# A merged schedule for a hybrid decoder trunk: MLP entry, down-projection and tail reordered, eight modulation tiles moved late

## The chip, the cores and the metric

One core of a Trainium2 chip runs the kernel. The time is the device time of one execution in microseconds (us), taken as the median of several; a profiled execution gives the trace from which everything else is read. The engines are TensorE (PE; weight loads are PEld), VectorE (DVE), ScalarE (ACT), GpSimd (POOL) and SyncE (SP), which here only issues DMA.

## The reference

One layer over 1024 tokens of width 1024, in float32. A conditioning vector gives six modulation vectors (shift, scale, gate for the mixer and for the MLP). The mixer joins causal pooling with chunked gated linear attention; then comes a gated MLP of 2 × 2816 channels with a causal convolution of width 3, and a last norm. Cut to what matters:

```python
mod = silu(c) @ ada_w + ada_b
sh1, sc1, g1, sh2, sc2, g2 = split(mod, 6)
h = rmsnorm(x) * (1 + sc1) + sh1
u, q, k, v, r, z = split(h @ w_in)
y = concat([pool_mixer(u), gla_mixer(q, k, v, r, z)]) @ w_out
x = x + g1 * y
h = rmsnorm(x) * (1 + sc2) + sh2
up = causal_conv3(h @ w_up) + conv_b
a, b = split(up, 2)
x = x + g2 * ((silu(a) * b) @ w_down)
out = rmsnorm(x) * final_norm
```

## The kernel before, in words

Channels lie on the 128 partitions, tokens along the free side, in two halves `hf` of 512 tokens (T = 512). Every large product is made of three fp32r matmuls per 128-channel block (high × high, high × low, low × high; `mm3`). For that each weight block is split on chip into a high part (a cast on ScalarE, L851) and a low part (a subtraction on VectorE, L852). All matmuls have line L107, so one goes by the names of their tiles: `pp` projections of the mixer, `gp` and `dg` gates and diagonal of the attention, `sc` its scores, `ss` sums of squares, `upx`, `upy`, `upz` the up-projection, `dn` the down-projection.

The order on TensorE is the order in which the code issues the matmuls. In the mixer this follows a clock of matmul time: side generators (`gates`, `gla_pair`, the norms) yield a delay in us of such time or a condition, and `tick` runs those that are due between the matmuls of the main jobs. The orders of the other engines and of SP's queue are made by the scheduling layer, within what data and buffers demand.

*Mixer.* `gates` (L317 on) makes from z the operand `le` (L320 to L322), yields 2.0, and then for each of two channel tiles does the product `gp`, a log-sigmoid on ScalarE and VectorE and a running sum `b` (L338). `gla_pair` begins, once `b`, k and q are there, with the differences of `b` on POOL (`le`, L359) and behind them the product of q and k on POOL (`le`, L402), which the diagonal product `dg` needs; then come exponentials on ScalarE (L363, L364), `kl` (L368) and `lq` (L371) on VectorE and the scores `sc`, over seven levels.

*Modulation.* 48 tiles of 128 × 1024 are loaded (512 KB each) and multiplied with the conditioning vector `cb`, spread over the partitions, by VectorE (L226), one sum per tile; a small operation (L232) stores it to `modv`. Tiles 16 to 47 run between the jobs of the mixer; the last eight, 40 to 47, are the gate of the MLP, which only the last residual sum uses (L1160).

*MLP up.* Each of 22 channel tiles takes seven products, numbered by kind (1, 2, 5, 6, 3, 7, 4), a scheme with sums and differences of the two token halves and of the two weight halves that needs seven products instead of eight. `order` is the list of steps (kind, i); the first RAMP = 6 tiles run kinds 1 and 2 before the rest. Step 4 ends a tile: convolution on VectorE (L987), Silu (L1043), product (L1046), store to `gd`, and a difference or sum of the halves on POOL (L862 or L1054) for the down-projection. `cb` in these steps (L994) is a tile's convolution input, another thing than the conditioning vector.

*MLP down.* The same scheme over p = 1, 2 and 5 mixed, 6 and 3 mixed, 7, 4, each of NJ = 11 steps; a step is four outputs of three matmuls each. `prepare_d` loads and splits operands three steps ahead. At the last step of a p the four sums are added to the residual tiles `xs` (L1160) or held (`hold`), squares go to `acc`, and the last step is cut into two halves of 256 tokens, after which sums, root (L1196, L1197), outputs (L1210, L1207, L1208) and stores (L1212) follow.

*Activation tables.* A table load on ScalarE (L189) stands before the first use of another set of functions; `exp_ln` (L187) loads the set of exponential and logarithm after a given instruction, here after the last Silu.

Of the kernel before, what the change touches and what calls it, by code (L numbers as in the profile page):

```python
# [26 lines left out]
ALU = mybir.AluOpType  # L27
# [26 lines left out]
def trunk_kernel(ctx, tc, xT, ccol, adaT, vecs, w_start, w_z, w_qkru, w_v, w_g2, w_pool,  # L54
# [165 lines left out]
    def mod_tile(t, a=None, late=None):  # L220
# [4 lines left out]
        with later(late):  # L225
            dve.scalar_tensor_tensor(out=a, in0=a, scalar=1.0, in1=cb, op0=ALU.mult,  # L226
                                     op1=ALU.mult, accum_out=acc)
# [90 lines left out]
    def gates(pz, hf):  # L318
# [4 lines left out]
        yield 2.0  # L323
# [70 lines left out]
    def gla_pair(hf, ct):  # L394
        b, k, q2 = bt[hf][ct], kt[hf][ct], qbd[hf][ct]
        pre = gla_prep(b, k, q2, LEVELS[0])
        attn = tmp("la", shape=(P, 4, 2, P))
        av = attn.rearrange("p c e t -> p (c e) t")
        qk = tmp("le")
        for hd in range(2):  # L400
            rr = slice(hd * 64, hd * 64 + 64)
            pool_e.tensor_tensor(out=qk[rr], in0=k[rr], in1=q2[rr, hd], op=ALU.mult)  # L402
        yield 3.0
# [109 lines left out]
    def gla_half(hf):  # L513
        for ct in range(2):
            yield lambda: all(x[hf][c] is not None for x in (bt, qbd, kt)
# [139 lines left out]
    mods = iter(range(16, 48))  # L655
# [61 lines left out]
    def jobs_out(hf):  # L717
# [24 lines left out]
        def evac(d, pp):  # L742
# [3 lines left out]
            if hf and d >= 4:  # L746
                sums[d - 4] = up_pool.tile([P, T], F32, tag="a22", name="s1", bufs=10)
                dve.scalar_tensor_tensor(out=sums[d - 4], in0=x1[1][d],
                                         scalar=modv[:, 32 + d:33 + d], in1=x1[1][d - 4],
                                         op0=ALU.mult, op1=ALU.add)  # L750
# [3 lines left out]
            nacc[hf] = sumsq_step(nacc[hf], d, x1[hf][d], pool_e, True, own)  # L754
# [242 lines left out]
    def seeded(src, prime):  # L997
# [353 lines left out]
```

## Time and profile before

| | |
|---|---|
| median of three runs | 1041.66 us (1040.40 to 1043.34) |
| profiled execution | 1043.22 us, span 1041.2 us |
| busy share of the span | PE 96%, PEld 79%, DVE 82%, ACT 52%, POOL 16% |
| memory traffic | 154.21 MB, mean 148 GB/s |

The span runs from the first to the last event of the trace; 2.0 us of the execution lie outside it. A row of the timeline shows start, duration, engine, line, operation, output and inputs, shape and count; brackets give how long the engine stood idle before it and what ended that. Rows of a stage table give, for a stretch, its length, busy time and count of each engine, the clock granted to TensorE (1.00 is full), the share of DMA engine time and GB/s.

### The profile page before, as it was taken

What the parts mean: (1) busy time and instruction counts of PE and PEld (TensorE: products, weight loads), DVE (VectorE), ACT (ScalarE), POOL (GpSimd) and SP (SyncE); (2) the same over time, 40 slices, a digit from 0 to 9 for tenths busy, and PEclk for the clock granted to TensorE, in tenths of its full rate; (3) what the DMA queues carried; (4) which work ended last, traced back from release to release, by engine and by line L of the source; (5) the groups of instructions that cost most, each with busy time, mean ns of one, the idle gap of its engine ahead of it and who ended that gap; (6) DMA issues with size and microseconds to landing.
All of it is one profiled execution on the core that took longest, in us unless ns stands there. A gap on an engine that the chain in (4) does not pass through costs nothing.

```text
span 1041.2 us, 12710 instructions
## 1 busy us (share of the span) xinstructions
PE 1002.2 (96%) x4507; PEld 819.5 (79%) x4507; DVE 848.8 (82%) x1212; ACT 541.9 (52%) x870; POOL 166.6 (16%) x156
## 2 busy tenths in 40 slices
PE   8989989999999999999999999999999999999995
PEld 6768767787787768877888888888888788888874
DVE  7967996889997949999878787777776675987884
ACT  4365575443633737665555555555554544644542
POOL 0035112223041120011101101101001000200210
PEclk9989989999999999999999999999999999999998
DMA  9823321455487441333222322333234787223542
GB/s 365 292 101 122 111 72 62 142 182 191 167 289 242 158 167 59 102 121 142 102 91 92 121 105 107 113 112 111 101 111 155 281 270 244 90 93 107 194 155 81
DMA packets 60815, 154.21 MB, mean 148 GB/s; under 512 B 6768, under 2 KB 9936, under 8 KB 60752
## 3 DMA queue, kind: packets, MB, share of 16 engines
q1 hardware_dynamic: 53904, 133.91, 37.3%
q0 software_dynamic: 4928, 17.30, 4.3%
q10 hardware_dynamic: 1920, 2.20, 0.7%
q8 instruction: 35, 0.57, 0.2%
q14 instruction: 28, 0.23, 0.1%
HBM read 127.69 MB, written 25.69 MB: 147 GB/s over the span
## 4 chain that ended last, share of the span: by engine, by line
PE 76%; DVE 12%; ACT 4%; DMA 4%; issue 2%; POOL 1%; SPq 0%; POOLq 0%; ACTq 0%; DVEq 0%
PE dn L107 18%; PE pp L107 16%; PE upy L107 15%; PE upx L107 11%; PE upz L107 10%; PE sc L107 2%; PE pr L107 2%; DVE ada L226 1%; DVE wl L158 1%; DVE xs L852 1%; PE ss L107 1%; DVE la L388 1%; DVE us L534 1%; POOL le L359 1%; DMA ua<-in_w_up_dram 1%
## 5 line engine op out<-in xcount | busy, mean ns | idle before, releaser
L107 PE MATMUL dn<-xs 128*128 128x512 f32 (+1 forms) x480 | 112.5, 390 | 1.7 <-DVE xs L852 1.3
L107 PE MATMUL dn<-ws 128*128 128x512 f32 x456 | 106.8, 390 | 2.0 <-DVE xs L1160 2.0
L107 PEld LDWEIGHTS dn<-xs 128*128 128x128 f32 x480 | 89.5, 190 | 21.3 <-DVE xs L852 2.1
L107 PEld LDWEIGHTS dn<-ws 128*128 128x128 f32 x456 | 85.8, 188 | 20.2 <-issue 2.4
L158 DVE TENSOR_TENSOR wl<-raw,wh 128x1024 fp32r<-128x1024 f32 (+1 forms) x49 | 62.6, 1277 | 31.9 <-ACT wh L156 31.8
L107 PE MATMUL upy<-sh,xs 128*128 128x512 f32 x264 | 86.6, 390 | 2.0 <-DVE cb L994 2.0
L107 PE MATMUL upy<-sh,ws 128*128 128x512 f32 x264 | 86.5, 390 | 0.0
L852 DVE TENSOR_TENSOR xs<-ua,xs 128x512 fp32r<-128x512 f32 x78 | 60.7, 783 | 14.8 <-ACT xs L851 14.8
L1047 POOL DMA_DIRECT2D gd<-y x22 | 12.0, 545 | 376.9 <-DVE y L1046 359.9
L156 ACT CAST wh<-raw 128x1024 fp32r<-128x1024 f32 (+1 forms) x49 | 50.4, 1029 | 39.5 <-PE pp L107 10.7
L107 PE MATMUL pp<-hh,wh 128*128 128x512 f32 x168 | 70.1, 417 | 0.5 <-ACT hh L285 0.5
L107 PE MATMUL pp<-hh,wl 128*128 128x512 f32 x168 | 66.7, 397 | 1.3 <-DVE wl L158 1.3
L852 DVE TENSOR_TENSOR ws<-ua,ws 128x512 fp32r<-128x512 f32 x76 | 55.3, 730 | 15.4 <-ACT ws L851 15.4
L107 PE MATMUL pp<-hl,wh 128*128 128x512 f32 x168 | 66.7, 397 | 0.5 <-DVE hl L287 0.4
L851 ACT CAST ws<-ua 128x512 fp32r<-128x512 f32 x76 | 47.1, 622 | 34.0 <-PE upy L107 17.3
L851 ACT CAST xs<-ua 128x512 fp32r<-128x512 f32 x78 | 48.1, 622 | 30.5 <-PE upy L107 17.4
L107 PE MATMUL upx<-hh,xs 128*128 128x512 f32 x192 | 63.3, 395 | 0.0
L862 DVE TENSOR_TENSOR ua<-ua 128x512 f32<-128x512 f32 x88 | 60.3, 690 | 2.1 <-DMA ua<-in_w_up_dram 0.2
L107 PE MATMUL upz<-sh,ws 128*128 128x512 f32 x184 | 60.4, 390 | 0.0
L987 DVE SCALAR_TENSOR_TENSOR y<-ca,vec,y 128x1023 f32<-128x1023 f32 (+1 forms) x44 | 56.4, 1281 | 4.4 <-ACT y L984 3.5
L107 PEld LDWEIGHTS upy<-sh,xs 128*128 128x128 f32 x264 | 49.6, 188 | 13.0 <-DVE cb L994 2.8
L987 DVE SCALAR_TENSOR_TENSOR y<-cb,vec,y 128x1023 f32<-128x1023 f32 (+1 forms) x44 | 56.3, 1280 | 2.4 <-ACT y L984 2.1
(259 smaller groups left out, 2482.5 us busy)
## 6 DMA issues: line engine op xcount, KB each, us to landing
ua<-in_w_up_dram SPq DMA_DIRECT2D x49, 512.0 KB, 3.3
ada<-in_adaT_dram SPq DMA_DIRECT2D x32, 512.0 KB, 3.3
gd<-y POOLq DMA_DIRECT2D x22, 512.0 KB, 2.9
da<-gd SPq DMA_DIRECT2D x36, 256.0 KB, 2.9
da<-in_w_down_dram SPq DMA_DIRECT2D x36, 256.0 KB, 3.3
raw<-in_w_qkru_dram SPq DMA_DIRECT2D x17, 512.0 KB, 3.5
raw<-in_w_out_dram SPq DMA_DIRECT2D x16, 512.0 KB, 4.1
x<-in_xT_dram SPq DMA_DIRECT2D x24, 256.0 KB, 4.2
```

Source lines behind the costliest of these rows:

```text
L107: pe.matmul(out=out, lhsT=lhsT, rhs=rhs, start=start, stop=stop, skip_group_check=more)
L156: act.copy(out=wh, in_=raw)
L158: mark["wl"] = dve.tensor_tensor(out=wl, in0=raw, in1=wh.bitcast(F32), op=ALU.subtract)
L226: dve.scalar_tensor_tensor(out=a, in0=a, scalar=1.0, in1=cb, op0=ALU.mult, op1=ALU.mult, accum_out=acc)
L359: pool_e.tensor_tensor(out=e.rearrange("p (n h) -> p n h", n=nb), in0=b.rearrange("p (n h) -> p n h", n=nb), in1=bb[:, :, 0, h - 1:h].broa ...
L388: dve.copy_predicated(out=av.rearrange("p a (n two h) -> p a n two h", two=2, h=h)[:, :, :, 1], mask=cit[:, mi].rearrange("p (n h) -> p n ...
L534: dve.tensor_tensor(out=n[:, lo:], in0=a[:, lo:], in1=a[:, lo - sh:16 + T - sh], op=ALU.add)
L851: act.copy(out=h, in_=src)
L852: dve.tensor_tensor(out=l, in0=src, in1=h.bitcast(F32), op=ALU.subtract)
L862: eng.tensor_tensor(out=out, in0=a, in1=b, op=ALU.subtract)
L987: dve.scalar_tensor_tensor(out=y[:, sh:], in0=c[:, :S - sh], scalar=cw[j], in1=y[:, sh:], op0=ALU.mult, op1=ALU.add)
L1047: nc.gpsimd.dma_start(out=gd[i], in_=ya)
```

## The change

It joins several edits.

- `gates` yields 3.0 in the first half and 4.5 in the second. `gla_pair` does the product of q and k before it waits for `b`.
- In the output projection of the second half the four sums follow the last tile, and the last adds of squares are on VectorE. Modulation tiles 40 to 47 no longer run in the mixer; `cb` is stored to memory. The Silu table is loaded after the second norm's exponential.
- In the MLP step (4, i − 1) stands one product later. Silu and what follows are kept back (`gated`) until the copy that seeds a later tile; differences and sums are on VectorE instead of POOL, those of the first six tiles from reloaded products.
- In the down-projection the exponential table is loaded after p = 1's held copies; `cb` and the eight tiles are loaded and multiplied from step 8 on (`late_mods`); p = 4's operands are loaded six steps ahead into buffers of their own; residual sums are formed as soon as an output is ready (`done`).
- In the tail the last two steps are cut in two halves, all of the first before the second; four of the eight outputs of a half are made by one 4 × 256 operation from tiles scaled before, and no output is made on ScalarE or POOL.

POOL at the start of the attention of the first half; `le<-k,lb` is the product of q and k, `le<-b` the differences of `b`. Before:

```order
L304 MEMSET lb 64x512
L359 ISA
L359 TENSOR_TENSOR le<-b 128x512
L402 TENSOR_TENSOR le<-k,lb 64x512 x2
L415 TENSOR_TENSOR lm<-b 128x512
L359 TENSOR_TENSOR le<-b 128x512 x2
```

and now:

```order
L304 MEMSET lb 64x512
L399 ISA
L399 TENSOR_TENSOR le<-k,lb 64x512 x2
L359 TENSOR_TENSOR le<-b 128x512 x2
L417 TENSOR_TENSOR lm<-b 128x512
L241 TENSOR_TENSOR nsa<-nsa,nsq 128x512
```

The product has moved ahead of the first operation on `b`.

VectorE in p = 1 of the down-projection; `xs` and `ws` are splits of the operands `ra`, `rb` and `da` of coming steps, `ada` the modulation products. Before:

```order
L852 TENSOR_TENSOR xs<-rb,xs 128x512
L852 TENSOR_TENSOR ws<-ra,ws 128x512
L852 TENSOR_TENSOR ws<-rb,ws 128x512
L862 TENSOR_TENSOR ra<-da,ra 128x512
L862 TENSOR_TENSOR rb<-rb_6958,rb 128x512
L852 TENSOR_TENSOR ws<-ra,ws 128x512
L852 TENSOR_TENSOR ws<-rb,ws 128x512
```

and now:

```order
L858 TENSOR_TENSOR ws<-rb,ws 128x512
L226 SCALAR_TENSOR_TENSOR ada,macc<-ada,cb 128x1024
L858 TENSOR_TENSOR ws<-ra,ws 128x512
L232 SCALAR_TENSOR_TENSOR modv<-macc,vec 128x1
L226 SCALAR_TENSOR_TENSOR ada,macc<-ada,cb 128x1024
L858 TENSOR_TENSOR xs<-da,xs 128x512 x2
L232 SCALAR_TENSOR_TENSOR modv<-macc,vec 128x1
L226 SCALAR_TENSOR_TENSOR ada,macc<-ada,cb 128x1024
L858 TENSOR_TENSOR ws<-rb,ws 128x512
```

The first modulation products stand between the splits of the last steps of p = 1 and of the first of p = 2.

TensorE at the end of the kernel; `ss<-acc` is the sum of the squares collected so far and `ss<-sq` that of one output tile. The difference, with − for before and + for now:

```order
 L107 MATMUL dn<-ws 128x512 x24
-L107 MATMUL dn<-xs 128x512 x12
-L107 MATMUL dn<-xs 128x256 x12
+L107 MATMUL dn<-xs 128x256 x42
 L107 MATMUL ss<-acc,ones 128x256
-L107 MATMUL dn<-xs 128x256 x12
+L107 MATMUL dn<-xs 128x256 x6
+L107 MATMUL ss<-sq,ones 128x256 x2
 L107 MATMUL ss<-acc,ones 128x256
-L107 MATMUL ss<-sq,ones 128x256 x8
```

All 48 products of the last two steps are now 256 wide, the first half's sum stands six matmuls ahead of the last product, and eight sums of single tiles have become three.

The diff, cut to its core:

```diff
-        yield 2.0
+        yield 4.5 if hf else 3.0
...
     def gla_pair(hf, ct):
-        b, k, q2 = bt[hf][ct], kt[hf][ct], qbd[hf][ct]
-        pre = gla_prep(b, k, q2, LEVELS[0])
-        attn = tmp("la", shape=(P, 4, 2, P))
-        av = attn.rearrange("p c e t -> p (c e) t")
+        k, q2 = kt[hf][ct], qbd[hf][ct]
         qk = tmp("le")
         for hd in range(2):
             rr = slice(hd * 64, hd * 64 + 64)
             pool_e.tensor_tensor(out=qk[rr], in0=k[rr], in1=q2[rr, hd], op=ALU.mult)
+        yield lambda: bt[hf][ct] is not None
+        b = bt[hf][ct]
+        pre = gla_prep(b, k, q2, LEVELS[0])
...
-    mods = iter(range(16, 48))
+    mods = iter(range(16, 40))
...
-            nacc[hf] = sumsq_step(nacc[hf], d, x1[hf][d], pool_e, True, own)
+            nacc[hf] = sumsq_step(nacc[hf], d, x1[hf][d], dve if hf and d >= 4 else pool_e,
+                                  True, own)
+            if hf and d == 7:
+                for e in range(4):
...
+    cbd = tc.dram_tile([P, NK * P], F32, name="cbd")
+    nc.sync.dma_start(out=cbd, in_=cb)
...
-    run_jobs(jobs_out(0), 2)
+    run_jobs(jobs_out(0), 1)
...
     for i in range(NFF):
-        order += [(1, i)] if i >= RAMP else [(5, i)]
-        order += [(4, i - 1)] if i else []
-        order += [(5, i), (2, i)] if i >= RAMP else []
-        order += [(6, i), (3, i), (7, i)]
+        done = [(4, i - 1)] if i else []
+        if i < RAMP:
+            order += [(5, i), (6, i)] + done + [(3, i), (7, i)]
+        else:
+            order += [(1, i), (5, i)] + done + [(2, i), (6, i), (3, i), (7, i)]
...
         r = rstd_of(nacc[1], s2)
+        with tc.issue_after(mark["exp"].ins):
+            act.preload_act_table_set("silu_and_others")
...
-        for _ in range(2):
+        for _ in range(2 if n else 0):
             next(second, None)
...
+    def gated():
+        while pend:
+            i, ya, yb = pend.pop(0)
+            with tc.issue_after(mark["seed"].ins):
+                act.activation(out=ya, in_=ya, func=AF.Silu)
+            dve.tensor_tensor(out=ya, in0=ya, in1=yb, op=ALU.mult)
             nc.gpsimd.dma_start(out=gd[i], in_=ya)
+            if RAMP <= i < 2 * RAMP:
+                a, b = small("s3"), small("s3")
+                nc.sync.dma_start(out=a, in_=gd[i - RAMP][:, 0:T])
+                nc.sync.dma_start(out=b, in_=gd[i - RAMP][:, T:])
+                sub(dve, a, a, b)
+                nc.gpsimd.dma_start(out=s3d[i - RAMP], in_=a)
...
+    def load_ahead(n):
+        if n < len(steps) and steps[n][0] == 4:
+            j = steps[n][1]
+            ahead[j] = blk("a4"), blk("b4")
+            ld(ahead[j][0], a_src(22, j))
+            ld_b(ahead[j][1], 21, j)
...
+        if p == 1:
+            last = hold(1, d, pp)
+            if d == 3:
+                exp_ln(last)
...
+    def finish_half(lo, order):
+        n = T // 2
         ss = bank("ss")[:, 0:n]
+        for d in order:
+            sq = acc[1][:, lo:lo + n] if d is None else acc[d, lo]
+            mm(ss, ones, sq, d == order[0], d == order[-1])
+        r = rstd_out(ss, n)
+        o = dn["o"].tile([P, 4, n], F32, tag="o", name="o", bufs=4)
+        dve.tensor_tensor(out=o, in0=xs_tail[:, :, lo:lo + n],
+                          in1=r.unsqueeze(1).broadcast_to([P, 4, n]), op=ALU.mult)
+        store(nc.scalar if lo else nc.sync, 1, 4, 4, lo, n, o)
+        outputs(1, lo, n, r, 0, 4)
...
+    def late_mods():
+        def big(name):
+            return dn["o"].tile([P, NK * P], F32, tag="o", name=name, bufs=4)
+        c = big("cb")
+        ld(c, cbd)
+        got = []
+        for t in range(40, 48):
+            a = big("ada")
+            ld(a, adaT[t])
+            got.append((t, a))
+            if len(got) < 3 and t < 47:
+                continue
+            yield
+            t1, a1 = got.pop(0)
+            mod_tile(t1, a1, c=c)
+            yield
```

More of the change, by code (lines that the diff above doesn't have):

```diff
@@ L514, in gla_half @@
         for ct in range(2):
-            yield lambda: all(x[hf][c] is not None for x in (bt, qbd, kt)
+            yield lambda: all(x[hf][c] is not None for x in (qbd, kt)
                               for c in ((ct,) if hf else (0, 1)))
@@ L1166, in down_mm @@
         ah, al = flat(ah), flat(al)
+        if p == 7 and 3 <= j < 7:
+            evac(1, j + 1, held[5, j - 3])
+        if p == 4 and j < 4:
+            x = xs[1][4 + j]
+            act.activation(out=x, in_=x, func=AF.Copy, scale=vec[:, V_FN + 4 + j:V_FN + 5 + j])
         if p in (1, 5) and j == 0:
@@ L1170, in down_mm, with hold, done @@
         more = p not in (1, 5)
-        cuts = ((0, T // 2), (T // 2, T // 2)) if p == 4 and j == NJ - 1 else ((0, T),)
-        for lo, n in cuts:
-            for d in range(4):
-                mm3(pp[d][:, lo:lo + n], bh[:, d], bl[:, d], ah[:, lo:lo + n], al[:, lo:lo + n],
-                    not more and j == 0, j == NJ - 1, more)
-            if n < T:
-                finish_last(pp, lo, n)
-        return pp
+        for d in range(4):
+            mm3(pp[d], bh[:, d], bl[:, d], ah, al, not more and j == 0, j == NJ - 1, more)
+            if j == NJ - 1:
+                done(p, d, pp[d], 0, T)
+    held = {}
+    def hold(p, d, pp):
+        held[p, d] = dn["o"].tile([P, T], F32, tag="hold", name="hold", bufs=8)
+        return act.copy(out=held[p, d], in_=pp)
+    def done(p, d, pp, lo, n):
+        if p == 1:
+            last = hold(1, d, pp)
+            if d == 3:
+                exp_ln(last)
+        elif p == 5:
+            hold(5, d, pp)
+        elif p == 2:
+            evac(0, d, pp)
+            act.copy(out=pp, in_=held[1, d])
+            squares(0, d)
+        elif p == 6:
+            evac(0, 4 + d, pp)
+        elif p == 3:
+            evac(0, 4 + d, pp)
+            squares(0, 4 + d)
+        elif p == 7:
+            evac(1, 4 + d, pp)
+            squares(1, 4 + d)
+        else:
+            sq = acc[d, lo] = square(evac(1, d, pp, lo, n), "sq", n)
+            if d < (1 if lo else 4):
+                a = acc[1][:, lo:lo + n]
+                dve.tensor_tensor(out=a, in0=a, in1=sq, op=ALU.add)
     acc = {}
@@ L1248, in trunk_kernel @@
     for n in range(EARLY, len(steps)):
-        prepare_d(n + 3)
+        p, j = steps[n]
+        load_ahead(n + 6)
+        if n >= 8:
+            next(late, None)
+        if j < NJ - 1:
+            prepare_d(n + 3)
         if n >= 2 * NJ - 2 and n % 2 == 0 and x_loads:
@@ L1252, in trunk_kernel @@
             ld(xs[hf][d], x1d[hf][d])
[L1253 to L1254 removed]
+        if p < 5 and p > 3 and j >= NJ - 2:
+            continue
+        down_mm(p, j)
+        if j == NJ - 1:
+            prepare_d(n + 3)
         if (p, j) == (7, 3):
             finish_first()
[L1257 to L1280 removed]
+    finish_last()
 def _tiles(w):
```

128 lines of the change are left out of this document (57 added, 71 removed).

## The prediction

> **What bounds the kernel now.** I read the page first, then the busy time by stage, then each place where TensorE stands still. The page's first rows, its clock row and the shares of the chain:
>
> ```profile
> PE 1002.2 (96%) x4507; PEld 819.5 (79%) x4507; DVE 848.8 (82%) x1212; ACT 541.9 (52%) x870; POOL 166.6 (16%) x156
> PEclk9989989999999999999999999999999999999998
> PE 76%; DVE 12%; ACT 4%; DMA 4%; issue 2%; POOL 1%; SPq 0%; POOLq 0%; ACTq 0%; DVEq 0%
> ```
>
> TensorE sets the end: it is idle for 1041.2 − 1002.2 = 39.0 us, and it runs below full clock here and there. An edit that leaves the matmuls nearly as they are can win only those 39 us and what the low clock costs. The stages (columns: length, then busy time of PE, PEld, DVE, ACT, POOL, the granted clock, DMA share, GB/s):
>
> ```profile
> 60.00:110.00 50.00, 46.62 (x219) 38.48 (x218) 39.74 (x46) 28.50 (x53) 27.16 (x20) 0.93 0.28 96
> 110.00:200.00 90.00, 82.71 (x399) 66.94 (x397) 75.17 (x129) 52.18 (x89) 18.07 (x17) 0.96 0.26 91
> 600.00:806.00 206.00, 206.00 (x911) 170.72 (x910) 156.90 (x191) 109.18 (x163) 26.55 (x33) 1.00 0.32 115
> 826.00:976.00 150.00, 150.00 (x659) 123.89 (x659) 120.18 (x182) 74.53 (x132) 13.22 (x7) 1.00 0.50 166
> 1024.00:1041.20 17.20, 6.30 (x37) 5.43 (x35) 8.65 (x22) 6.01 (x14) 1.45 (x2) 0.82 0.37 122
> ```
>
> The long stretches of the MLP have no idle TensorE at all, with VectorE at 157 of 206 and 120 of 150 us. So an operation moved to VectorE there has cover, and nothing is to be won there. What can be won is in the mixer, at the seams and in the tail. Narrow windows show the low clock, each right behind a stop of TensorE:
>
> ```profile
> 72.50:79.20 6.70, 6.70 (x19) 5.45 (x20) 6.70 (x9) 4.36 (x9) 4.58 (x4) 0.50 0.12 39
> 147.60:154.30 6.70, 5.64 (x13) 4.48 (x14) 6.25 (x12) 3.85 (x8) 0.00 (x0) 0.50 0.20 73
> 386.50:389.80 3.30, 3.30 (x6) 1.66 (x5) 2.36 (x4) 0.50 (x1) 0.00 (x0) 0.50 0.34 103
> 823.40:826.70 3.30, 3.30 (x10) 2.54 (x9) 2.88 (x5) 0.36 (x1) 0.00 (x0) 0.50 1.02 395
> ```
>
> At half clock a busy us does half a us of work, so these cost 3.35, 2.8, 1.65 and 1.65 us: half of the PE column. A stop that goes takes its half-clock stretch with it.
>
> **The change, part by part.** Gains are negative.
>
> *First half, gates and q·k.* Rows of the timeline (start, duration, engine, line, operation; in brackets the idle time before it and what ended it):
>
> ```profile
> 62.50 0.50 PE L107 MATMUL gp<-le,g2w 96*128 96x512 f32 x1 [0.81 <-ACT le L322]
> 67.43 1.87 POOL L359 TENSOR_TENSOR le<-b 128x512 f32<-128x512 f32 x1 [17.17 <-DVE b L338]
> 69.26 2.68 POOL L402 TENSOR_TENSOR le<-k,lb 64x512 f32<-64x512 f32 x2
> 70.74 1.75 DVE L371 TENSOR_TENSOR lq<-lb,le 128x512 f32<-128x512 f32 x1
> 71.99 1.27 PE L107 MATMUL dg<-hsel,le 128*128 128x2 f32 x7 [2.58 <-POOL le L402]
> ```
>
> The product that `dg` waits for (2.68) stands on POOL behind an operation that needs `b` and comes after a 17.17 us wait. Moved ahead of it, it needs only k and q; POOL has nothing else then, so it is done well before 67. `gp`, three matmuls later, meets its operand. That removes 0.81 + 2.58 + 3.35 = 6.7. What is late next: the scores `sc`, which need `lq`, ready at 70.74 + 1.75 = 72.5. Without its stops TensorE comes there at about 70.8: `gp` at 62.5, then 35 full matmuls at 0.224 (36.00 us for 161 records at 862 to 898, below) and the small `dg`. `lq` itself should be quicker when POOL is quiet, so I leave a stop of about 1.3 and a part of a half-clock stretch: −4.5, between −1.5 and −6.7.
>
> *Second half.*
>
> ```profile
> 148.04 0.57 ACT L322 CAST le<-pp 32x512 fp32r<-32x512 f32 x1
> 148.66 0.80 PE L107 MATMUL gp<-le,g2w 96*128 96x512 f32 x1 [2.66 <-ACT le L322]
> 168.77 0.51 PE L107 MATMUL pp<-wh,hh 128*128 128x512 f32 x1 [1.73 <-ACT k L312]
> ```
>
> `gp` waits for a cast queued on ScalarE behind other work. The gate now yields 4.5 instead of 2.0, and in the built order `gp` stands 16 matmuls (3.6 us) later, more than the 2.66 stop. At most −(2.66 + 2.8) = −5.5; at worst the same queue stops the next product and nothing is won. Nearer the first, since other matmuls fill the place: −4.0. The 1.73 at 168.77 is a k copy behind the queue of the exponentials; with POOL's work in another order it goes or stays: −1.0 (0 to −1.7).
>
> *Sums of the second half of the residual, and the second norm.*
>
> ```profile
> 384.32 1.58 POOL L241 TENSOR_TENSOR nsa<-nsa,nsq 128x512 f32<-128x512 f32 x1 [0.38 <-ACT nsq L237]
> 385.95 1.60 PE L107 MATMUL ss<-nsa,ones 128*128 128x512 f32 x2 [2.23 <-POOL nsa L241]
> ```
>
> The last adds go to VectorE, the four sums behind them, and `ss` stands twelve matmuls later (2.7 us), more than its 2.23 wait. Gain 2.23 + 1.65 = 3.9; I take −3.6 (0 to −3.9). The preload of the Silu table costs 1.28 on ScalarE (row below) ahead of the ramp's products, which have that much room.
>
> *Gated products of the MLP.*
>
> ```profile
> 459.34 2.20 DVE L852 TENSOR_TENSOR xs<-ua,xs 128x512 fp32r<-128x512 f32 x1
> 459.67 1.30 POOL L862 TENSOR_TENSOR y<-y 128x512 f32<-128x512 f32 x1
> 462.19 0.50 PE L107 MATMUL upy<-sh,xs 128*128 128x512 f32 x1 [1.13 <-DVE cb L994]
> 476.93 0.50 PE L107 MATMUL upy<-sh,xs 128*128 128x512 f32 x1 [0.85 <-DVE cb L994]
> ```
>
> While POOL subtracts, VectorE's split takes 2.20 instead of 0.68 (the same form at 994.19, below). All 22 such POOL operations go to VectorE, where the same work costs 0.69 (993.58, below): 15 us over the 425 us of the MLP's up part, which has a quarter of VectorE free. The six earliest products are read back from memory (12 loads of 256 KB), at some 110 GB/s of traffic. Step (4, i−1) comes one product later, which also gives `cb` time. −1.8 (0 to −2.0); +4 if the cover were gone (six stops of 0.69).
>
> *Start of the down-projection.*
>
> ```profile
> 818.72 1.28 ACT L189 ACT_TABLE_LOAD   x1
> 820.02 0.62 ACT L851 CAST xs<-rb 128x512 fp32r<-128x512 f32 x1
> 820.69 0.73 PE L107 MATMUL dn<-xs 128*128 128x512 f32 x2 [0.37 <-ACT xs L851]
> 822.72 2.82 PE L107 MATMUL dn<-xs 128*128 128x512 f32 x7 [1.30 <-DVE xs L852]
> ```
>
> The table load stands between the last Silu and the cast that TensorE waits for, and POOL's last add slows the split. The load moves behind p = 1, where nothing waits for it; the cast comes 1.28 earlier. All is 0.37 + 1.30 + 1.65 = 3.3; −3.0 (0 to −3.3).
>
> *Start of p = 4.*
>
> ```profile
> 993.58 0.69 DVE L862 TENSOR_TENSOR da<-da,rb 128x512 f32<-128x512 f32 x1 [0.98 <-DMA da<-in_w_down_dram]
> 994.19 0.68 DVE L852 TENSOR_TENSOR xs<-da,xs 128x512 fp32r<-128x512 f32 x1
> 995.68 0.70 PE L107 MATMUL dn<-ws 128*128 128x512 f32 x2 [2.00 <-DVE xs L1160]
> ```
>
> VectorE's subtraction waits for a load, and the evacuation that frees a bank stands behind it. With the loads six steps ahead and evacuation first: −1.8 (+1 to −2.0).
>
> *The two-half tail.*
>
> ```profile
> 1026.25 0.59 PE L107 MATMUL ss<-acc,ones 128*128 128x256 f32 x2
> 1029.56 2.86 DVE L1210 SCALAR_TENSOR_TENSOR o<-xs,vec,r 128x256 f32<-128x256 f32 x7 [2.52 <-ACT r L1197]
> 1036.79 0.38 ACTq L1212 DMA_DIRECT2D out_dram<-o  x1
> ```
>
> From the end of the products (1026.25) both roots, then the output operations, 0.41 each (2.86 / 7), go one after the other, the last store is issued at 1036.8 and lands by 1041.2. In the change the first half's sum stands ahead of the last six narrow matmuls, so its root is there about 0.6 us after the products. VectorE then needs per half one 1024-wide product (1.2, as the 1.27 of the modulation row below) and four of 0.41: 5.7 in all, with some evacuations between. The last is done about 6.7 after the products, where the last store stood 10.5 after them: −3.8 (−2.5 to −4.5). Cutting a second step in two puts 24 more 256-wide matmuls for 12 fewer 512-wide: +0.2.
>
> *The eight modulation tiles.* Columns of the first row: busy, mean ns of one, idle before.
>
> ```profile
> L226 DVE SCALAR_TENSOR_TENSOR ada<-ada,cb 128x1024 f32<-128x1024 f32 x32 | 40.3, 1266 | 3.6 <-DMA ada<-in_adaT_dram 3.4
> 826.00:862.00 36.00, 36.00 (x158) 29.76 (x158) 26.33 (x43) 16.83 (x30) 0.00 (x0) 0.99 0.88 295
> 862.00:898.00 36.00, 36.00 (x161) 29.82 (x160) 26.08 (x42) 17.27 (x31) 1.27 (x1) 1.00 0.63 212
> 898.00:920.00 22.00, 22.00 (x99) 18.23 (x98) 22.00 (x32) 13.26 (x26) 5.78 (x3) 1.00 0.13 48
> ```
>
> They leave the mixer, where TensorE rarely waits for them: 0. In the built order they stand among the splits from p = 1 on, here about 826 to 862. There they add 8 × 1.27 = 10.1 us to VectorE (26.3 of 36 busy, so 36.4: full), and nine 512 KB loads, 4.7 MB, to a stretch that moves 295 GB/s × 36 us = 10.6 MB; at the 395 GB/s of 823 to 827 it could move 14.2, so 1.1 MB, 3 us, slides behind. Cover: operands are split three steps (8 us) ahead, part of those loads are residual tiles needed only at about 894, and 862 to 898 has 10 us of VectorE free. Queued behind a modulation that waits for its load are the splits of the coming steps, and behind the loads on SP the weights of p = 2 and 5. At 898 to 920 VectorE is full without any of it. Bounds: 0 with the cover, +11 without; I take +1.5, nearer the first.
>
> *At nothing:* the store of the conditioning vector (512 KB, in the mixer at 91 GB/s); the four rescaling copies in p = 4, on ScalarE at half its time (74.5 of 150); the outputs' issue on SP, which has by then no load left to issue. Without cover each is one operation of 0.6, or 1.7 for the store, once.
>
> **Sum:** −4.5 − 4.0 − 1.0 − 3.6 − 1.8 − 3.0 − 1.8 − 3.8 + 0.2 + 1.5 = −21.8. The profiled execution took 1043.2 (2.0 outside its span), so 1021.4 on its basis; the median of the runs shown is 1.56 below it: 1041.66 − 21.8 = 1019.9, say **1020 us**. My bounds of the terms, not all at once, make its own range 1011 to 1025.
>
> **Rivals.** *The mixer's stops only move.* Its late operand is then the next one: `lq` at 72.5, ScalarE's queue at 148. For: VectorE is busy 75 of 90 us at 110 to 200. Against: the operand waited for at 71.99 sits behind unrelated work. The 9.5 of the mixer shrink to 2: 1020 + 7.5 = 1027.
>
> *The tiles take VectorE's cover.* It enters 898 to 920, already 22.00 of 22, with a backlog of up to 10 us, and TensorE stands for that: about 1030. For: 36.4 of 36. Against: 862 to 898 has room to catch up.
>
> *Slower than before.* The same place, with the memory queue: each of the eight tiles brings a stop of the 1.27 modulation and a late 512 KB load (1.8 us at 295 GB/s). That is 3.1 us each, over the 2.2 us after which a half-clock stretch stood at 386, so 1.65 more: 8 × 4.7 = 38 us, 1020 − 1.5 + 38 = 1056. It decides only once VectorE's lead of three steps is used up.
>
> *The stops are not what lowers the clock.* The half-clock stretches then stay, and of the gains only the idle time remains: 3.35 + 2.8 + 1.65 + 1.65 = 9.5 less, about 1029. Against: all four stand right behind stops of 1.3 to 2.7 us. [...]
>
> **How the numbers follow.** Forecast 0.60, mixer's stops move 0.19, VectorE's cover 0.09, clock stays 0.04, slower 0.04, and 0.04 for more than the sum (the mixer's full 13.9 instead of 9.5, and the others at their far ends: 1009). Range 1009 to 1032. About 0.3%, 3 us, is what can be told from no change: faster 0.94, same 0.02, slower 0.04.
>
> **What would show it.** Right: `dg` with no wait for POOL and the clock at 1.00 from 72 to 79; no half clock at 386 and 823; `upy` without stops for `cb`; 826 to 976 without idle TensorE; the last store about 7 us behind the last product. Wrong: `sc` waiting 2 us or more for VectorE; `gp` still behind ScalarE; `dn` waiting for `xs` or `ws` splits around 840 to 920, with VectorE full and the modulations waiting for their loads.

## The result

The changed kernel takes 1026.17 us (median of 4 runs, 1024.54 to 1026.31), the kernel before beside it 1042.50 (4 runs, 1040.40 to 1044.39). The ratio is 0.984, with a 95% interval of 0.9818 to 0.9863: 16.3 us faster, where 1020 had been predicted, 21.7 us faster. The profiled execution of the change took 1026.08 us with a span of 1024.3.

First the rows of its page that answer to those of before: the engines' busy time and the clock.

```profile
PE 995.5 (97%) x4509; PEld 811.7 (79%) x4509; DVE 849.5 (83%) x1239; ACT 540.8 (53%) x871; POOL 128.0 (13%) x128
PEclk9999999999899999999999999999999999999998
```

TensorE is idle for 1024.3 − 995.5 = 28.8 us instead of 39.0, and the other 6.7 of the 16.9 us between the spans are busy time that fell, which is mostly less time at half clock: 6.8 us ahead of the tail instead of 23.9. Ahead of the tail the clock row has one digit below 9, the 8 of the slice from 256 to 282 us: that is the start of the out-projection, below. The group of the down-projection's weight products (busy, mean ns, then idle before) shows a waiter that it did not have: VectorE's weight splits.

```profile
L107 PE MATMUL dn<-ws 128*128 128x512 f32 x456 | 108.2, 391 | 2.2 <-DVE ws L858 2.1
```

The best ledger is by stages of TensorE's work, from the start of one product to the start of another as the timeline gives them (us):

| from … to | before | after | change | predicted |
|---|---|---|---|---|
| first `gp` … first out product `pp<-yh` | 205.69 | 196.56 | −9.1 | −9.5 |
| … first `upx` | 112.65 | 115.04 | **+2.4** | 0 |
| … first `upz` | 38.81 | 34.64 | −4.2 | −3.6 |
| … last `upz` | 383.76 | 381.03 | −2.7 | −1.8 |
| first `dn` … last `dn` | 219.79 | 220.85 | **+1.1** | −3.1 |
| last `dn` … end | 15.07 | 10.62 | −4.5 | −3.8 |

Two stages hold more than the whole miss: 2.4 lost in the out-projection, where nothing had been forecast, and 4.2 in the down-projection; the other four together gained 1.8 more than forecast. The stages of the change (columns as before the prediction's stage table):

```profile
60.00:110.00 50.00, 46.50 (x232) 37.75 (x232) 41.03 (x53) 29.53 (x56) 28.82 (x20) 1.00 0.30 96
110.00:200.00 90.00, 88.53 (x436) 71.36 (x435) 79.62 (x132) 55.44 (x96) 18.63 (x18) 1.00 0.33 108
200.00:270.00 70.00, 63.59 (x298) 51.71 (x297) 64.61 (x109) 33.08 (x57) 16.47 (x9) 0.96 0.54 175
...
812.00:848.00 36.00, 36.00 (x161) 29.81 (x160) 31.78 (x61) 18.21 (x31) 0.00 (x0) 1.00 0.96 349
848.00:884.00 36.00, 36.00 (x161) 29.81 (x160) 29.22 (x47) 16.22 (x29) 1.38 (x1) 1.00 0.83 279
884.00:906.00 22.00, 20.59 (x90) 16.51 (x89) 22.00 (x32) 13.41 (x26) 5.67 (x3) 1.00 0.38 130
906.00:962.00 56.00, 54.72 (x234) 42.79 (x233) 49.58 (x76) 23.36 (x43) 6.16 (x4) 1.00 0.52 165
```

From 60 to 200 the clock is full. In 200 to 270 it is 0.96 and 6.4 us are idle. In the down-projection TensorE keeps its pace until 884, beside a VectorE that has to do 31.78 of 36, and loses it in the next 22 us, where VectorE is full. The count of matmuls says more there than the idle time, since a matmul behind a stop is drawn longer (0.50 us in several rows below, where the mean of the group above is 391 ns): it is compared below.

**The start of the attention.** Rows of TensorE and POOL:

```profile
61.10 2.61 POOL L399 TENSOR_TENSOR le<-k,lb 64x512 f32<-64x512 f32 x2 [10.73 <-ACT k L312]
...
66.66 0.95 PE L107 MATMUL dg<-hsel,le 128*128 128x2 f32 x8
...
72.23 1.16 PE L107 MATMUL sc<-lq,kl 128*128 128x128 f32 x8 [0.38 <-DVE lq L371]
...
78.70 1.16 PE L107 MATMUL sc<-lq,kl 128*128 128x128 f32 x8 [1.19 <-DVE lq L371]
...
88.06 2.02 DVE L158 TENSOR_TENSOR wl<-raw,wh 128x1024 fp32r<-128x1024 f32 x1 [2.45 <-ACT wh L156]
...
90.14 0.50 PE L107 MATMUL pp<-wl,hh 128*128 128x512 f32 x1 [1.32 <-DVE wl L158]
```

The product of q and k is done at 63.7 and `dg` waits for nothing. The scores wait twice for `lq`, and a weight split that takes 2.02 beside POOL's sums of squares stops TensorE for another 1.32.

**The start of the out-projection.** ScalarE and then TensorE:

```profile
263.41 1.28 ACT L453 ACT_TABLE_LOAD   x1
264.70 0.58 ACT L529 COPY us<-pp 128x512 f32<-128x512 f32 x1
...
265.34 0.80 PE L107 MATMUL pp<-yh,wh 128*128 128x512 f32 x1 [3.96 <-ACT us L529]
```

The copy that frees the bank of this product (the piece of accumulator memory that it fills) has a table load ahead of it on ScalarE. In the kernel before, the same product waited too, at 270, but there the table load stood behind the copy:

```profile
271.44 0.67 ACT L552 ACTIVATE yh<-po,vec 128x512 fp32r<-128x512 f32 x1
272.01 0.57 ACT L527 COPY us<-pp 128x512 f32<-128x512 f32 x1
...
273.55 1.28 ACT L451 ACT_TABLE_LOAD   x1
...
272.63 0.50 PE L107 MATMUL pp<-yh,wh 128*128 128x512 f32 x1 [2.24 <-ACT us L527]
```

**The down-projection at 885.** VectorE, TensorE and POOL:

```profile
885.21 1.79 DVE L858 TENSOR_TENSOR ws<-ra,ws 128x512 fp32r<-128x512 f32 x1
886.92 1.75 DVE L858 TENSOR_TENSOR ws<-rb,ws 128x512 fp32r<-128x512 f32 x1
888.60 1.77 DVE L858 TENSOR_TENSOR ws<-ra,ws 128x512 fp32r<-128x512 f32 x1
...
888.73 2.56 PE L107 MATMUL dn<-ws 128*128 128x512 f32 x10 [1.17 <-DVE ws L858]
...
882.62 7.20 POOL L1254 TENSOR_TENSOR acc<-acc,sq 128x512 f32<-128x512 f32 x3 [73.39 <-ACT sq L1246]
```

Three splits in a row take 1.77 instead of 0.68 while POOL adds squares, and TensorE waits for them.

**The tail.** VectorE's last outputs and the last stores:

```profile
1018.53 1.67 DVE L1272 SCALAR_TENSOR_TENSOR hold<-xs,vec,r 128x256 f32<-128x256 f32 x4
...
1019.44 1.38 SPq L1263 DMA_DIRECT2D out_dram<-hold  x2
```

The last `dn` began at 1013.69 and the last store is issued by 1020.8: 7 us, as forecast.

### The profile page after: what moved, and what is told of

Same layout as the page of the kernel before. It is cut to its first block, busy times and chain, and to the rows that moved or that the text cites. A ratio compares the mean times of both kernels' runs of the same rounds, so it can differ in the third digit from the quotient of the medians.

```text
span 1024.3 us, 12716 instructions
## 1 busy us (share of the span) xinstructions
PE 995.5 (97%) x4509; PEld 811.7 (79%) x4509; DVE 849.5 (83%) x1239; ACT 540.8 (53%) x871; POOL 128.0 (13%) x128
## 4 chain that ended last, share of the span: by engine, by line
PE 64%; DVE 17%; DMA 8%; issue 4%; ACT 3%; POOL 2%; SPq 1%; DVEq 0%; POOLq 0%; ACTq 0%
PE upy L107 18%; PE upx L107 12%; PE upz L107 12%; PE pp L107 10%; PE dn L107 9%; DMA ada<-in_adaT_dram 2%; DVE wl L158 2%; DMA da<-in_w_down_dram 2%; DVE ada L226 2%; PE pr L107 2%; DVE ws L858 2%; DVE xs L858 1%; DVE rb L868 1%; POOL le L359 1%; ACT wh L156 1%
## 5 line engine op out<-in xcount | busy, mean ns | idle before, releaser
L156 ACT CAST wh<-raw 128x1024 fp32r<-128x1024 f32 (+1 forms) x49 | 50.3, 1027 | 30.5 <-PE pp L107 11.3
L858 DVE TENSOR_TENSOR xs<-ua,xs 128x512 fp32r<-128x512 f32 x78 | 53.0, 687 | 14.5 <-ACT xs L857 14.5
L858 DVE TENSOR_TENSOR ws<-ua,ws 128x512 fp32r<-128x512 f32 x76 | 52.0, 688 | 14.6 <-ACT ws L857 14.6
L107 PE MATMUL pp<-yh,wh 128*128 128x512 f32 x128 | 53.8, 421 | 4.3 <-ACT us L529 4.0
L107 PEld LDWEIGHTS upy<-sh,ws 128*128 128x128 f32 x264 | 49.5, 188 | 10.3
```

What stands on the lines that cost most here:

```text
L107: pe.matmul(out=out, lhsT=lhsT, rhs=rhs, start=start, stop=stop, skip_group_check=more)
L156: act.copy(out=wh, in_=raw)
L858: dve.tensor_tensor(out=l, in0=src, in1=h.bitcast(F32), op=ALU.subtract)
```

## The experiments

Times are medians, with the lowest and highest run; ratios are to the kernel before, run in turn on the same chip. Its own median was between 1042.5 and 1044.8 in the different sets, so runs of different sets (the change; e1 to e4; e5 to e8; e9 to e11; e12) compare by their ratios.

| run | us | ratio, 95% interval |
|---|---|---|
| the change | 1026.17 (1024.54–1026.31) | 0.984 [0.9818, 0.9863] |
| e1 | 1021.15 (1020.28–1023.31) | 0.9791 [0.9755, 0.9826] |
| e2 | 1021.64 (1019.69–1023.29) | 0.979 [0.9746, 0.9833] |
| e3 | 1023.36 (1020.83–1024.91) | 0.9806 [0.9769, 0.9843] |
| e4 | 1026.89 (1025.86–1029.48) | 0.9846 [0.981, 0.9883] |
| e5 | 1033.50 (1032.58–1036.36) | 0.9915 [0.9885, 0.9945] |
| e6 | 1023.91 (1023.05–1025.37) | 0.9823 [0.9798, 0.9848] |
| e7 | 1019.52 (1019.14–1020.68) | 0.9783 [0.9754, 0.9812] |
| e8 | 1024.75 (1022.98–1027.82) | 0.9833 [0.9802, 0.9863] |
| e9 | 1025.43 (1023.67–1027.01) | 0.9811 [0.9788, 0.9835] |
| e10 | 1019.44 (1018.69–1020.28) | 0.9755 [0.9737, 0.9773] |
| e11 | 1019.59 (1017.26–1020.29) | 0.9751 [0.9727, 0.9776] |
| e12 | **1013.30** (1012.62–1013.52) | **0.9714** [0.9685, 0.9743] |

### What the eight tiles cost in the down-projection: e1, e2, e7

e1 puts tiles 40 to 47 back into the mixer: behind each job of the first half of the out-projection run two modulation tiles instead of one. The store of `cb` to memory and the late loads are undone too.

```diff
-    mods = iter(range(16, 40))
+    mods = iter(range(16, 48))
-    run_jobs(jobs_out(0), 1)
+    run_jobs(jobs_out(0), 2)
-        if n >= 8:
-            next(late, None)
```

> The changed kernel (1026.2 us) with one part undone: the eight modulation tiles 40 to 47 are again loaded and multiplied in the mixer, two tiles per job of the first output projection; everything else as in the change. Theory A (the tiles, their loads and VectorE products, eat the lead of the operand splits): the stops of TensorE from 880 to 960 us in the changed kernel, 5.4 us in all over full pace, fall below 1 us, and the output projection gets back at most 1 us of small stops: 1021 to 1023 us. Theory B (the stops come from the residual sums and the early evacuations, which stand in another order now): they stay, 1025.5 to 1028 us.

e2 leaves the tiles late and moves the ten adds of squares of the down-projection from POOL to VectorE.

```diff
-            pool_e.tensor_tensor(out=acc[hf], in0=acc[hf], in1=sq, op=ALU.add)
+            dve.tensor_tensor(out=acc[hf], in0=acc[hf], in1=sq, op=ALU.add)
```

> The changed kernel with one line changed: the ten sums of squares of the down-projection are on VectorE instead of POOL. Theory A (a POOL operation slows the VectorE splits beside it: 1.75 to 1.79 us at 885 to 889 us instead of 0.68, so each POOL addition costs VectorE more than the 0.69 of doing it itself): the splits beside are back at 0.68, the stop of 1.4 us at 887 goes, 1023 to 1025 us. Theory B (VectorE is simply full there, 22.00 of 22 us): ten operations more make the stops longer, 1027 to 1030 us.

e7 is e2 with the same for the sums of squares of the mixer's two norms (`nsa`).

```diff
-            sumsq_step(nacc["n1"], k, xin(1, k), pool_e)
+            sumsq_step(nacc["n1"], k, xin(1, k), dve)
-            nacc[hf] = sumsq_step(nacc[hf], d, x1[hf][d], dve if hf and d >= 4 else pool_e,
+            nacc[hf] = sumsq_step(nacc[hf], d, x1[hf][d], dve,
```

> The changed kernel with all sums of squares on VectorE instead of POOL: those of the down-projection, as in the run that took 1021.6 us, and those of both norms in the mixer. Theory A (a POOL addition slows VectorE beside it by more than its own 0.69): the stops for wl at 88 to 91 us (1.8 us together) and for ss at 327 (0.9) go, 1017.5 to 1020.5 us. Theory B (VectorE is the tight engine of the mixer, so 20 more operations there cost more than they save): 1022 to 1026 us.

Stages of e1 that answer to 884 to 962 of the change, then those of e7:

```profile
883.00:905.00 22.00, 22.00 (x97) 17.94 (x96) 22.00 (x32) 12.55 (x24) 4.67 (x3) 1.00 0.34 110
905.00:961.00 56.00, 55.73 (x243) 45.14 (x242) 51.07 (x78) 26.05 (x46) 6.17 (x4) 1.00 0.57 178
```

```profile
884.00:906.00 22.00, 22.00 (x99) 18.07 (x98) 22.00 (x38) 13.05 (x24) 0.00 (x0) 1.00 0.44 144
906.00:962.00 56.00, 56.00 (x247) 46.03 (x246) 51.47 (x85) 26.65 (x47) 0.00 (x0) 1.00 0.53 172
```

In the same 78 us the change made 90 + 234 = 324 matmuls, e1 340 and e7 346: at 36.00 / 161 = 0.224 each, 3.6 and 4.9 us. From the first to the last `dn` it is 220.85 in the change, 216.00 in e1, 215.29 in e2 and 215.17 in e7. So the tiles cost 4.9 us against +1.5 forecast. But e2 and e7 keep them and lose nothing: the price is neither the tiles' alone nor POOL's alone. As I read it, the tiles use up lead of the splits before 884, and behind that the splits that POOL stretches find TensorE at their heels. The traces show a small loss of lead: at the start of the same matmul of the down-projection, the change had finished one split fewer than e1 (67 against 68 at 870 us, 75 against 76 at 886). VectorE is full in this stretch in all of them (22.00 of 22). In e7 it does 38 operations there, six more than the 32 of the change, and is not later. The splits of e2, with an add between them:

```profile
885.85 0.69 DVE L1254 TENSOR_TENSOR acc<-acc,sq 128x512 f32<-128x512 f32 x1
886.46 0.68 DVE L858 TENSOR_TENSOR ws<-ra,ws 128x512 fp32r<-128x512 f32 x1
```

An add of 0.69 on VectorE costs VectorE less than the 1.1 (1.77 − 0.68) by which POOL's add lengthens a split. e7 also won 1.9 us in the mixer (first `gp` to first out product 194.61), where the waits at 77 and 88 to 90 were gone.

### The stop at the start of the out-projection: e3, e4, e6, e9

Two causes were held against each other: VectorE is late there with modulation products ahead of the pooling, or the Silu table load stands ahead of the copy. e3 runs no modulation tiles behind the last two projection jobs of the second half (`mods_each` may be a tuple).

```diff
-                             ("u0 u1 u2 u3", 2)):
+                             ("u0 u1 u2 u3", (2, 2, 0, 0))):
-    run_jobs(jobs_out(0), 1)
+    run_jobs(jobs_out(0), 2)
```

> The changed kernel with four modulation tiles moved from behind the last two pooling projections (u2, u3) of the second half to the first output projection. It aims at the stop of 3.96 us at 261 us and the 6.83 us at half clock behind it, which in the kernel before were 2.24 and 3.41. Theory A (VectorE's modulation products and their late loads stand ahead of the pooling sums that ScalarE's cast waits for, so the copy that frees the bank is late): the stop falls to 2 us or less, half clock to 3.4 us or nothing, 1021.5 to 1024 us. Theory B (ScalarE's table load ahead of that copy made the difference): the table load still stands ahead of it, the stop stays above 3.5 us, 1025.5 to 1027 us.

e4 makes the table load and the activations behind it wait for the last pooling copy (`mark["u13"]`), and the cast of the first out weight as well.

```diff
+            yield lambda: rt[hf][3] is not None and (hf == 0 or "u13" in mark)
+            with tc.issue_after(normed[hf].ins), later(mark["u13"] if hf else None):
...
+                return split_w(raw, (P, 2, T), mark["u13"] if hf == 0 and i == 0 else None)
```

> The changed kernel with the order on ScalarE changed at the same stop: the copy of the last pooling projection stands ahead of the Silu table load and of the next weight cast. Theory B (the table load, 1.28 us, made the difference): the stop at 261 us falls from 3.96 to 2.7 us or less and one of the two half-clock windows goes: 1022.5 to 1025 us. Theory A (the chain of VectorE behind it sets the time): the copy still waits for the cast of the pooled difference in ScalarE's order; the stop falls by no more than the 1.28 us and half clock stays at 6.8 us: 1024.5 to 1026.5 us.

e6 does the same with the cast of the second out weight (`i == 1`) in place of the first.

> As the run before that put the last pooling copy ahead of the Silu table load, but with only the second weight cast behind the copy, so the first output product has its weights in time. Theory B (the table load, 1.28 us, ahead of the copy made the stop at 261 us longer than in the kernel before): the stop falls from 3.96 to about 2.5 us and half clock from 6.83 to 3.41 us: 1022.5 to 1024 us. Theory A (VectorE's chain sets the time): the stop falls by less than 0.5 us: 1025 to 1027 us.

e9 leaves the table load and fills the bank that the copy frees last, so that the other three banks of the first out product come ahead of it.

```diff
+                grid = [(j, n) for j in range(2) for n in range(4)]
+                if hf == 0 and i == 0:
+                    grid.sort(key=lambda t: t[1] == 3)
```

> The changed kernel (1026.2 us) with one edit: in the first output product the fourth bank, the one that the last pooling copy frees, is filled after both weight blocks of the other three, nine matmuls (2.0 us) later. Theory (the stop at 261 us is the wait for that bank and nothing else, and what it costs beyond its length is half clock in the next window of 3.41 us, which follows a window that TensorE spent idle for about half or more): the stop falls from 3.96 to about 1.9 us, half clock from 6.83 to 3.41 us or, if the stop is split over two windows, to nothing: 1020.5 to 1023 us. Rival (the split of the next weights is late too, so the stop only moves): 1025 to 1027 us.

TensorE's stop in e3, e4, e6 and e9 (two rows), each from the timeline of its own run:

```profile
265.58 0.75 PE L107 MATMUL pp<-yh,wh 128*128 128x512 f32 x1 [3.58 <-ACT us L529]
```

```profile
263.42 0.80 PE L107 MATMUL pp<-yh,wh 128*128 128x512 f32 x1 [4.37 <-ACT wh L156]
```

```profile
264.55 0.50 PE L107 MATMUL pp<-yh,wh 128*128 128x512 f32 x1 [2.53 <-ACT us L529]
```

```profile
266.42 0.50 PE L107 MATMUL pp<-yh,wh 128*128 128x512 f32 x1 [1.92 <-ACT us L529]
...
294.52 0.77 PE L107 MATMUL pp<-yh,wh 128*128 128x512 f32 x1 [3.25 <-DVE x L747]
```

Without the modulations the stop is 3.58 instead of 3.96, so they are not its main cause (the out-projection gains 1.9; half clock still follows the stop, with products 0.43 us apart from 266.13 on, and the run's mean clock is 0.997 instead of 0.994). With the copy ahead of the table load it is 2.53, shorter by 1.43, near the 1.28 of the load, and the out-projection takes 112.84 instead of 115.04. e1, which was not made for this stop, says the same. There the table load stands behind the copy again, as in the kernel before, and the stop is 2.35 without half clock behind it (the products go on 0.23 us apart):

```profile
266.08 1.28 ACT L453 ACT_TABLE_LOAD   x1
...
265.16 0.50 PE L107 MATMUL pp<-yh,wh 128*128 128x512 f32 x1 [2.35 <-ACT us L529]
```

So what put the load ahead of the copy is the part that e1 undoes: the late tiles with the store of `cb`. Why it did is not shown. (The out-projection of e1 is no shorter than 113.82, since with the tiles in it stops of 1.61 and 0.60 stand at 293 to 295.) e4 says nothing on that, since my edit put the weight that the product needs behind the copy and made a wait of its own. e9 halves the stop and pays for it 28 us later, where the products wait for the residual addition on VectorE, with half clock behind it (a mean clock of 0.96 from 270 to 296): its out-projection takes 116.78, and whether its total is below that of the change the intervals don't tell.

### The mixer's gates: e5

e5 undoes `gates` and `gla_pair`: yield 2.0, and the product of q and k behind the wait for `b`.

```diff
-        yield 4.5 if hf else 3.0
+        yield 2.0
```

> The changed kernel (1026.2 us) with the mixer's part undone: the gates yield 2.0 again and the product of q and k stands again behind the wait for b. Theory A (these two edits removed the stops at 61, 69, 122, 145 and 166 us of the kernel before, some 9 us there after what is left of them): stops of 2 to 3 us for dg and gp come back with half clock behind them, 1034 to 1037 us. Theory B (the stops only moved to the scores and weight splits, so the edits won little): 1028 to 1031 us.

The old stops came back, at 62, 72, 147 and 167:

```profile
62.76 0.50 PE L107 MATMUL gp<-le,g2w 96*128 96x512 f32 x1 [0.81 <-ACT le L322]
...
72.24 1.05 PE L107 MATMUL dg<-hsel,le 128*128 128x2 f32 x8 [2.55 <-POOL le L402]
...
147.84 0.80 PE L107 MATMUL gp<-le,g2w 96*128 96x512 f32 x1 [2.67 <-ACT le L322]
...
167.85 0.50 PE L107 MATMUL pp<-wh,hh 128*128 128x512 f32 x1 [1.70 <-ACT k L312]
```

The stage from the first `gp` to the first out product takes 204.92 instead of 196.56, and the median is 7.3 us above that of the change (7.8 by the ratios), between the two expected ranges and nearer to the first: most of what the mixer's stops cost had not moved elsewhere, it was won. (My sum had 9.5.)

### The gated products: e8

e8 gives the differences and sums of tiles 6 to 21 back to POOL and keeps step (4, i − 1) one product later.

```diff
-                sub(dve, yb[:, 0:T], ya[:, 0:T], ya[:, T:])
+                sub(pool_e, yb[:, 0:T], ya[:, 0:T], ya[:, T:])
-                add_to(t, t, ya[:, T:])
+                pool_e.tensor_tensor(out=t, in0=t, in1=ya[:, T:], op=ALU.add)
```

> The changed kernel with the differences and sums of the gated products of tiles 6 to 21 back on POOL; the order of the steps and the delayed Silu stay. Theory A (the move off POOL removed the stops for cb of 1.13 and 0.85 us): stops of about 1 us per tile come back wherever a split stands beside, at least 2 us in all, 1028 us or more. Theory B (the later place of step 4 alone gives cb its time): no stop in the up part, 1025 to 1027 us.

TensorE's group with these products in e8, and two operations of one tile (VectorE, POOL):

```profile
L107 PE MATMUL upy<-sh,xs 128*128 128x512 f32 x264 | 86.3, 389 | 0.0
```

```profile
525.12 1.38 DVE L858 TENSOR_TENSOR ws<-ua,ws 128x512 fp32r<-128x512 f32 x1
...
524.63 1.30 POOL L868 TENSOR_TENSOR y<-y 128x512 f32<-128x512 f32 x1
```

POOL stretches the split again, to 1.38, and no product waits for `cb`: for tiles 6 to 21 the move off POOL won nothing. But e8 does not say what removed the two stops of the kernel before. They stood at 462 and 477, where step 4 of tiles 2 and 3 was due, and with the operations of tiles 6 to 21 on POOL that kernel had no stop either. For the first six tiles e8 leaves POOL without these operations, so there the later step, the kept-back Silu and the move off POOL are not told apart.

### Together: e10, e11, e12

e10 joins e7, e6 and e9. e11 is e10 with the tiles back in the mixer.

> Four edits together: all sums of squares on VectorE (1019.5 us alone), the last pooling copy ahead of the second weight cast and the Silu table load (1023.9 alone), the fourth bank later. If the gains of different places add: 1019.5 less the stop at 261 us and its half clock (3.94 and 3.41/2 in the first of these), so 1014.5 to 1016 us. If VectorE's added sums put the stop elsewhere in the mixer: 1017 to 1020 us.

> As the run with the four edits, and with the eight modulation tiles back in the mixer. With the sums on VectorE the down-projection had no stop left with the tiles in it, so moving them back wins nothing there; the first output projection takes eight products of 1.22 us on VectorE more. Theory A (either remedy is enough): the same or up to 3 us slower than the run with the tiles late. Theory B (the tiles still cost something late): 1 to 2 us faster.

e12 is e10 with two more edits in the first half of the out-projection: in its first four jobs the loads of the residual rows come one job earlier, and no modulation tiles run behind these four jobs; the eight tiles run behind the last four, two each.

```diff
-                if kp == 2:
+                if kp == (1 if i < 4 and not hf else 2):
-    run_jobs(jobs_out(0), 1)
+    run_jobs(jobs_out(0), (0, 0, 0, 0, 2, 2, 2, 2))
```

> Edit: the kernel of e10 (all sums of squares on VectorE, last pooling copy and second weight cast ahead of the Silu table load, first out product's fourth bank later), and in addition, in the first half of the out-projection, the loads of the residual rows one job earlier, and the modulation tiles of the out-projection kept for its second half (0,0,0,0,2,2,2,2). In e10 a stop of 2.45 us stood at 287.4, before a product whose bank waited for the residual addition on VectorE. Theory A (that addition was late for its load and for the modulation product ahead of it): the stop goes, nothing takes its place before 330, 1016.5 to 1018.5 us. Theory B (VectorE is simply full from 250 to 300, so each remedy moves the stop): a stop of 1 us or more stands elsewhere between 255 and 350, and the time stays at 1019 to 1021 us.

Two stages and a stop of e10, then the same of e12:

```profile
255.00:275.00 20.00, 18.03 (x86) 14.50 (x86) 18.77 (x30) 14.44 (x22) 5.89 (x1) 1.00 0.40 134
275.00:300.00 25.00, 21.73 (x114) 17.73 (x113) 20.97 (x36) 9.23 (x17) 6.44 (x3) 1.00 0.75 251
...
290.29 0.47 PE L107 MATMUL pp<-yh,wh 128*128 128x512 f32 x1 [2.45 <-DVE x L753]
```

```profile
255.00:275.00 20.00, 20.00 (x101) 16.90 (x100) 17.73 (x27) 15.89 (x26) 5.02 (x2) 1.00 0.37 129
275.00:300.00 25.00, 23.01 (x119) 19.01 (x118) 23.06 (x41) 8.04 (x14) 1.65 (x2) 1.00 0.78 254
...
288.64 0.50 PE L107 MATMUL pp<-yh,wh 128*128 128x512 f32 x1 [1.13 <-DVE x L753]
```

e10 gained less than its parts: no more than e7 alone by the medians, 3 us more by the ratios, whose intervals overlap. Its out-projection took 115.29, as long as that of the change (115.04). e11 against e10 shows no gain: 214.51 instead of 215.83 in the down-projection, where one remedy already sufficed, and 116.62 in the out-projection, where the tiles now stand in the way. e12 is the best of all: 2.9% below the kernel before, where the change is 1.6% below it, and about 13 us faster than the change. Its out-projection takes 110.72. The stop of 2.45 became two, of 0.86 and 1.13, so it moved as one theory had it; but the time fell below what the other had asked for, since two stops of e10 at 261 to 266, of 0.50 and 1.47, are gone too. VectorE there was not simply full: with the same operations in another order TensorE waited less. How much of this the earlier loads gave, and how much the modulations kept for later, was not told apart.

## Why the prediction was right, and where not

*Right in sign and within its range, with 5.4 us too much expected.* The range was wide because of the rivals. The time lies just outside the 1011 to 1025 that the sum allowed itself, and nearer to the 1027 of the rival by which the mixer's stops only move than to 1020. That nearness is chance: e5 shows the stops of the mixer won, and the miss stands in other stages. The low ends don't come out of the terms either: all of them at their best give −29.4, or 1012.3, not 1011 or 1009. By its own steps:

- **First half, gates and q·k**, −4.5: the stops fell from 0.81 + 2.58 and 3.35 of lost clock to 0.38 + 1.19 + 0.48 + 1.32 and 0.13, so −3.2. The mechanism holds (e5). The prediction had named `lq` as late next, with 1.3; what it left out is that POOL, done with the product of q and k, goes on with sums of squares beside `lq` and the weight splits. e7 takes these away and wins 1.9 in the mixer.
- **Second half, `gp`**, −4.0: a wait of 0.13 at `gp` and 0.86 at the scores are left of 2.66 + 2.8, so −4.5. **k copy**, −1.0: the whole 1.73. The stage as a whole: −9.1 against −9.5, which is so close in part by chance, since stops that the sum did not name changed as well: 1.30 at 124 went, 1.59 at 199 fell to 0.48, and 0.41 at 243 grew to 1.17.
- **Sums and second norm**, −3.6: −4.2 by the stage, no wait and no half clock. Right.
- **Gated products**, −1.8: all stops gone, −2.7 by the stage, a little more than forecast. Which of its two reasons counted, the stretched split or the later step, stays open: e8 leaves the tiles with the stops as they are in the change.
- **Start of the down-projection**, −3.0: one wait of 0.57 remains, no half clock. **Start of p = 4**, −1.8: no wait. Both right.
- **Tail**, −3.8: −4.5.
- **The eight tiles**, +1.5 between 0 and +11: 4.9 (e1). This is the mis-sized term. The sum of VectorE's work was right (26.3 + 10.1 = 36.4 forecast; 31.78 and 29.22 of 36 in the two stretches into which the tiles fell), but it was taken as work that catches up by 898. The prediction's own row showed VectorE full from 898 to 920 and its own rival named the place; it missed that three splits there, for which TensorE would wait at once, are lengthened by 1.1 us each by POOL, an effect that it had priced for the gated products (2.20 instead of 0.68) and did not carry over. e1 adds that it was not 0 in the mixer either: the tiles' leaving put the table load of the next point in the way.
- **Nothing named at 270**: the Silu table load that stood in front of the last copy, together with the stop that was there before. The stage lost 2.4. The stop itself went from 2.24 to 3.96, and the half clock behind it from one stretch of 3.41 to two. With the load behind the copy again the stop is 2.53 (e6) or 2.35 (e1), so the load's place accounts for nearly all of the 1.72 by which it grew. The stop that was there before stays, and whether half clock follows it differs: in e6 the products are 0.43 us apart from 265.95 on, in e1 0.23. The prediction weighed ScalarE's table loads at the start of the down-projection and ahead of the ramp, but not this one, whose lines the change leaves as they were.

The rival that the mixer's stops only move fell with e5. The rival of VectorE's cover was true in half: the place and the wait, at half the price and with POOL as its second condition. That half clock is not due to the stops fell too: where stops went, it went (the clock of the change is 1.00 from 60 to 264 and from 271 to the last `dn`).

## What to carry to other kernels

When work is moved onto an engine, look not at its mean load behind the move but at the next stretch where it is full, and at what lengthens its operations there: here another engine's adds, which cost the full engine 1.1 us each, more than the 0.69 of doing them itself. A stop that a change doesn't touch still belongs into the sum, since the order of the queues around it changes. And when a stop moves from remedy to remedy, sort the work of the engine behind it by who needs it first, as e12 did, before calling the engine full.

## What the runs showed of the hardware

**Half clock came in steps of 3.41 us.** In the traces of before and of the change the stretches of half clock ahead of the tail last 3.41 or 6.83 us. Those of before start at 72.44, 147.54, 273.83, 386.47 and 823.38, so 22, 37, 33 and 128 times 3.41 from one to the next. Two windows by these steps of the kernel before, and two of e5, at the same stop of `dg` (those of e5 are counted back from its half clock at 148 to 156, where a mean clock of 0.67 makes 5.3 us at half, up to 153.3):

```profile
69.07:72.48 3.41, 0.83 (x7) 0.49 (x5) 2.70 (x3) 1.85 (x4) 3.26 (x4) 0.99 0.39 154
72.48:75.89 3.41, 3.41 (x12) 2.93 (x12) 3.41 (x4) 1.88 (x4) 3.24 (x4) 0.50 0.08 23
```

```profile
67.99:71.41 3.42, 1.71 (x8) 1.08 (x6) 2.69 (x4) 1.82 (x4) 3.35 (x3) 1.00 0.46 152
71.41:74.82 3.41, 2.58 (x15) 2.32 (x16) 3.41 (x3) 1.19 (x3) 3.33 (x3) 1.00 0.00 1
```

A stop of 2.58 inside one window was followed by half clock; a stop of 2.55 cut by a border into 1.71 and 0.83 was not. In the traces of before and of the change, from 60 us to the last `dn`, the four full-clock windows with 2.22 to 2.68 us of idle TensorE were followed by half clock. Of those with less, the one of 1.67 and one of 1.53, both of before, were; the two of 1.64, one in each kernel, and all with up to 1.38 were not. At half clock products of 128x512 stood 0.43 us apart (e5, 148.43 to 150.99), at full 0.23. So of two stops of about the same length one cost half clock and one did not, and a saving or loss of 1.7 to 3.4 us, by my estimate half of one stretch of 3.41 or of 6.83, can be chance.

**VectorE's longer operations ended with POOL's.** In the traces of before and of the change each of the 42 and 19 additions, subtractions and products of 128x512 on VectorE that took over 0.85 us stood beside a POOL operation and ended 0.55 to 0.56 us after it; the others took 0.66 to 0.82. The split of e8 above agrees (525.12 + 1.38 = 526.50, against 524.63 + 1.30 = 525.93, with rounded digits). So the length of these operations went by the end of POOL's; why is not shown. POOL's were longer as well: the three adds of the row at 882.62 took 7.20, so 2.40 each, where a POOL operation of that shape took 1.30 in the row at 524.63.
